# A two-layer hybrid decoder on one core: parameters loaded behind the eighth block of x, the first four blocks singly, and separate accumulators for the last group's row halves

## The chip, the cores and the metric

The kernel runs on one core of a Trainium2 chip. The metric is the device time of one execution in microseconds (us); of several runs the median is given. Engines are called as in the profile: PE (TensorE) with its weight loads PEld, DVE (VectorE), ACT (ScalarE), POOL (GpSimd), and SP, whose queue issues most of the DMAs.

## The reference

Two layers, each of 256 tokens of width 2048, all in float32. A layer is one wide input projection, three mixers on its columns, one output projection, and a LayerNorm of the residual sum:

```
for l in range(DEPTH):                          # DEPTH = 2
    u = x @ w_in[l]                             # 2048 -> 6080 columns
    (cb, cc, ch, cg, cq, ckv, kpe, mg, rcols, rg) = _split(u, IN_SIZES)
    y_conv = _short_conv_branch(cb, cc, ch, cg, conv_w[l])
    y_mla  = _mla_branch(cq, ckv, kpe, mg, ..., cos, sin)
    y_rwkv = _rwkv7_branch(rcols, rg, rwkv_mu[l], ...)
    mix = jnp.concatenate([y_conv, y_mla, y_rwkv], axis=-1)
    x = _layer_norm(DEEPNORM_ALPHA * x + mix @ w_out[l], ln_g[l], ln_b[l])
```

The RWKV branch first mixes each column with the token before it, `xs = cols + (shift(cols) - cols) * mu`, which needs the parameters `mu`.

## The kernel before, in words

Every product is made from two parts of each operand: a rounded "hi" (ACT copies the float32 value to fp32r) and a rest "lo" (DVE subtracts). `split_in` makes the pair; `split_w` does it for a weight block and appends the two instructions to the list `splits`. A product is then hi·hi, hi·lo and lo·hi (`mm3`, lines 341 to 343, or lines 441 and 443 where the hi and lo of x lie side by side and one matmul of 512 columns does two of the three).

The input projection is done in groups of 512 columns (`MAIN`: k, a, r, v, ...). In layer 0 the first group, k, is loaded with x: the 16 blocks of x (128 rows of the transposed x, 256 columns) lie in memory beside the 512 columns of k's weights, so one block of a `first` tile is 128 x 768 values, 384 KB. `STEPS` says which blocks make one load; `load_first` issues the load on SP's queue, and splits the x part, and `split_w` the weight part. In the first group these splits are chained in order on ACT and on DVE (`in_turn`). The `first` tiles lie in pool s8 of nine slots, four of which hold the split x; a tile waits for a free slot. Then come the groups a, r, v and so on, each in two halves: `in_group` takes one accumulator per half, makes 32 pairs of matmuls (L441, L443) into it, and evacuates it with an ACT copy and a DVE add.

Accumulators come from `acc`: pool pp in PSUM, tag "acc", two buffers of two banks each. The group k takes one, the first half of a the other, and the second half of a whichever is released first: k's, when the four `shift_mix` of `rwkv_k` have read it (tile kx, one ACT and one DVE instruction each), or the first half's own, when it is evacuated.

`shift_mix` needs parameters: `pars` (loaded) and `pc` (four DVE instructions made from it in `load_params`, here for both layers). `load_constants` loads `pars`, `cs`, `posi` and `ones` from POOL's queue, behind a one-element POOL copy that reads the last `first` tile, so that they start when that has landed.

The output projection (`out_proj`) has four groups of 512 columns. The last one is done in column halves i = 0 and 1 and row halves h = 0 and 1 (128 tokens each). In layer 0, `po[i][h]` for both h lay in one accumulator tile, one bank each: column half 0 is done for both h and then added to the residual; of column half 1, first h = 0 is multiplied, added (`add`) and its LayerNorm begun (`root`), then h = 1.

A planner writes the order of each engine's instructions (`schedule_with_timeline_sim=True`): it runs a model of time, takes at each point the ready instruction of the highest priority (`high_priority` raises it), and assigns buffers as they come free in that model. `after(a, b)` forces that a stands behind b. Within `tick`, DVE instructions of the mixers are also held behind a weight split further on (`gates`, by the counters `used` and `splits`).

Of the kernel before, what the change touches and what calls it, by code (L numbers as in the profile page):

```python
# [14 lines left out]
ALU = mybir.AluOpType  # L15
# [36 lines left out]
Q_CONV, Q_QG, Q_KVG, Q_MUR, Q_MUWA, Q_MUK, Q_MUV = 0, 12, 16, 18, 22, 23, 27  # L52
Q_W0, Q_A0, Q_KK, Q_KA, Q_RK, Q_GNG, Q_GNB, Q_LNG, Q_LNB = 31, 35, 39, 43, 47, 51, 55, 59, 75
# [58 lines left out]
def hybrid_layers(ctx: ExitStack, tc: tile.TileContext, x, positions, xT, w_in, w_out, w_uq, w_ukv, par, wa_in, gb_in,  # L112
# [13 lines left out]
    gates, splits = {}, []  # L126
# [18 lines left out]
    V, A, G, T = Gated(nc.vector, "V"), Gated(nc.scalar, "A"), nc.gpsimd, nc.tensor  # L145

    def after(inst, earlier):

        tc.add_manual_dep(inst.ins, earlier.ins.name,
                          mybir.DependencyInfo(mybir.DependencyClass.NoSync, mybir.DependencyReason.DATA),  # L150
                          reason="loads no earlier than needed")
# [9 lines left out]
    ones = cp.tile([P, 2 * P], F32R, tag="ones", name="ones")  # L161
# [5 lines left out]
    def load_constants(x):  # L167

        last = G.tensor_copy(pars[0:1, 0, 0:1], x[0:1, 0:1])
        for to, src in ((pars, par), (cs, cst), (posi, positions[0:1, :].to_broadcast([P, S]))):  # L170
            load = nc.gpsimd.dma_start(to, src)
            after(load, last)
            last = load
        o32 = c4("ones32", (P, 2 * P))
        load = nc.gpsimd.dma_start(o32, sums)
        after(load, last)
        V.tensor_copy(ones, o32)
        loaded.append(load)

    def zeros(rows):  # L180

# [2 lines left out]
    params, loaded, mark = [], [], {}  # L184
# [4 lines left out]
    def s4(name, shape=(P, 4, S), dt=F32):  # L189
        return slot("s4", name, shape, N4, dt)  # L190

    def c4(name, shape=(P, 4, S), dt=F32):
        return slot("c4", name, shape, NC4, dt)

    def s8(name, shape=(P, 8, S), dt=F32):
        return slot("s8", name, shape, N8, dt)


    def pair(name):
        return s8(name, (P, 2, 4, S), F32R)  # L200
# [4 lines left out]
    def split_in(hi, lo, src):  # L205
        a = A.copy(hi, src)
        v = V.tensor_tensor(lo, src, hi.bitcast(F32), ALU.subtract)
        if not params:
            in_turn("A", a)
            in_turn("V", v)  # L210
        return a, v
# [1 line left out]
    xres = x  # L213
    xs = [pair(f"x0_{g}") for g in range(4)]

    STEPS = [(0, 1), (1, 1), (2, 2), (4, 2), (6, 2), (8, 2), (10, 2), (12, 2), (14, 2)]

    def load_first(k0, n):

        t = s8(f"first{k0}", (P, n, S + 512))  # L220
        in_turn(1, nc.sync.dma_start(t, xT[:, k0:k0 + n, :]))
        with tc.high_priority():
            to, at = xs[k0 // 4], k0 % 4
            split_in(to[:, 0, at:at + n, :], to[:, 1, at:at + n, :], t[:, :, 0:S])
        if k0 == 14:
            load_constants(t[:, 0, :])
        return t[:, :, S:].rearrange("p k (i c) -> p i k c", i=2)

# [2 lines left out]
    def in_turn(queue, load):  # L231
        if queue in turn:
            after(load, turn[queue])
        turn[queue] = load
# [13 lines left out]
    def load_params(l):  # L248
        pq = pars[:, l, :]
        pc = cp.tile([P, 29], F32, tag=f"pc{l}", name=f"pc{l}")  # L250
        V.tensor_scalar(pc[:, 0:13], pq[:, Q_MUR:Q_MUR + 13], -1.0, 1.0, ALU.mult, ALU.add)
        V.tensor_scalar(pc[:, 13:21], pq[:, Q_W0:Q_W0 + 8], 0.5, None, ALU.mult)
        V.tensor_scalar(pc[:, 21:25], pq[:, Q_KA:Q_KA + 4], 0.5, None, ALU.mult)
        V.tensor_scalar(pc[:, 25:29], pq[:, Q_KA:Q_KA + 4], -0.5, 1.0, ALU.mult, ALU.add)
        col = lambda j: pq[:, j:j + 1] if j < NQ else pc[:, j - NQ:j - NQ + 1]
        return dict(col=col, om=NQ - Q_MUR, hw=NQ + 13, ha=NQ + 17, hk=NQ + 21, ok=NQ + 25)

# [95 lines left out]
    def acc(name):  # L353

        return pp.tile([P, 2, 512], F32, tag="acc", name=name)
# [21 lines left out]
    def wide_steps(l):  # L377
        return [(k, 2) for k in range(0, NKC, 2)] if l else STEPS

# [23 lines left out]
    def weights(name, k0):  # L403
        while len(asked) < LOOK:
            asked.append(load())
        load()
        return ready.pop((name, k0))
# [805 lines left out]
    def ln_rows(l):  # L1213

        t = sm.tile([P, 2, 16], F32, tag="lnp", name=f"lnp{l}", bufs=1)
        load = nc.gpsimd.dma_start(t, gbp[l])
        after(load, loaded[0])
        hi = sm.tile([P, 2, 16], F32R, tag="lnh", name=f"lnh{l}", bufs=1)
        lo = sm.tile([P, 2, 16], F32R, tag="lnl", name=f"lnl{l}", bufs=1)
        V.tensor_copy(hi, t)  # L1220
        V.tensor_tensor(lo, t, hi.bitcast(F32), ALU.subtract)
        rows = dr.tile([5, D], F32R, tag=f"lnr{l}", name=f"lnr{l}")
        for i, src in enumerate((hi[:, 0], lo[:, 0], hi[:, 0], hi[:, 1], lo[:, 1])):
            nc.gpsimd.dma_start(rows[i].rearrange("(p i) -> p i", p=P), src)
        return rows

    def out_proj(l, ms, xres, last, begin, lnr):
# [52 lines left out]
        def part1(at, n):  # L1280
            z = zs[0][:, 1, at:at + n]
            return V.scalar_tensor_tensor(z, z, rstd[:, 1:2], gs[0][:, 1, at:at + n], ALU.mult, ALU.add)
# [59 lines left out]
        for g in range(4):  # L1342
            xr = c4(f"xr{l}_{g}", (P, 2, 512))
            after(nc.scalar.dma_start(xr, xres[0, :, g * 512:(g + 1) * 512].rearrange("(h p) c -> p h c", p=P)), begin)
            zs.append(xr)
            gt = s4(f"gb{l}_{g}", (P, 2, 512))
            after(nc.scalar.dma_start(gt, gb_in[l:l + 1, :, g * 512:(g + 1) * 512].to_broadcast([P, 2, 512])), begin)
            gs.append(gt)
            if g < 3:
                pa = acc(f"po{l}_{g}")  # L1350
                po = [pa[:, h, :] for h in range(2)]
                for k0 in ORDER:
                    ws = [weights(f"wo{l}_{g}", k0 + k) for k in (0, 2)]
                    for h in range(2):
                        part(po, h, 512, ws)
                for h in range(2):
                    add(po[h], g, 0, 512, h, g)
                continue
            po, held = [], {}
            for i in range(2):  # L1360
                pa = acc(f"po{l}_{g}_{i}")
                po.append([pa[:, h, 0:256] for h in range(2)])
                held[i] = []
                for k0 in ORDER:
                    held[i].append(weights(f"wo{l}_3_{i}", k0))
                    if not last and i == 0:
                        for h in range(2):
                            part(po[i], h, 256, held[0][-1:])
                if not last and i == 0:
                    for h in range(2):  # L1370
                        add(po[i][h], g, 0, 256, h, 3)
            cts = []

            def turn_row(h):
                ct, m = row(h)
                cts.append(ct)
                return m

            first_rows = {AT[last][0]: lambda: turn_row(0),
                          AT[last][1]: lambda: [norm(0, g_, cts[0])[0] for g_ in range(4 if last else 1)][-1]}  # L1380
            for h in range(2):
                for i in range(2):
                    if not last and i == 0:
                        continue
                    part(po[i], h, 256, held[i], first_rows if h and i else {})
                    add(po[i][h], g, i * 256, 256, h, 3 + i)
                mark.setdefault(l + 1, []).append(root(h))
            if not last:
                xs += [pair(f"x{l + 1}_{g}") for g in range(1, 4)]
            keep_warm()  # L1390
            if last:
                turn_row(1)
                part1(256, 256)
                nc.scalar.dma_start(rows(0)[:, 1], zs[0][:, 1])
                for g_ in range(1, 4):
                    norm(1, g_, cts[1], ((0, 512),) if g_ < 3 else ((0, 256), (256, 256)))
            else:
                turn(1, 0, ((0, 2),))
                t = turn(0, 0, hold=mark[l + 1][1])
                after(part0(256, 256), mark[l + 1][1])  # L1400
                mark[l + 1][1] = t
                part1(256, 256)
                nc.gpsimd.dma_start(rows(0), zs[0])
                turn(1, 0, ((2, 2),))
                turn_row(1)
                run(rest(cts))
                tick()
# [3 lines left out]
    for l in range(L):  # L1411
        u, t = {}, {}
# [55 lines left out]
```

## Time and profile before

| | |
|---|---|
| median of 3 runs | 908.29 us (908.03 to 909.82) |
| the profiled execution | 909.28 us |
| its span in the trace | 907.5 us |
| PE busy | 893.1 us, 98% of the span |
| DVE, ACT, POOL busy | 687.5, 486.1, 24.6 us |
| TensorE clock granted, mean | 0.994 |

The profiled execution lies 1.78 us above its span, and 0.99 us above the median. "Busy" for PE counts the matmuls whatever their clock; a stage at the half clock is busy twice as long.

### The profile page before, as it was taken

The numbers are of one execution on the slowest core, as the hardware profiler recorded it, in microseconds if no ns is written. First come the engines' busy times: TensorE is split into PE (matmuls) and PEld (weight loads), VectorE is DVE, ScalarE is ACT, GpSimd is POOL, SyncE is SP. The second block draws the span as 40 slices with busy tenths as digits, with TensorE's granted clock in tenths as the row PEclk, the third lists the DMA queues.
The fourth block names the chain that finished last, engine by engine and source line by source line (L and its number), as shares of the span: only waits on it lengthen the run. The fifth ranks groups of instructions, "written<-read, shape, count | busy, mean of one in ns | idle before, by whom it ended". The sixth has DMA issues, their size and how long they took to land.

```text
span 907.5 us, 16003 instructions
## 1 busy us (share of the span) xinstructions
PE 893.1 (98%) x6314; PEld 786.7 (87%) x6314; DVE 687.5 (76%) x1166; ACT 486.1 (54%) x752; POOL 24.6 (3%) x47
## 2 busy tenths in 40 slices
PE   8899999999999999999999999999999999999996
PEld 8788888888889888888898888888888998988896
DVE  7677988986558987476775889799765699875665
ACT  6577546444447666544246874564444575765430
POOL 2120000000000000000020000000000000000000
PEclk9989999999999999999999999999999999999999
DMA  9755674666535654696576456646654456547832
GB/s 373 222 139 161 185 208 130 187 197 177 161 111 165 193 161 118 205 325 204 171 225 194 136 190 191 170 124 204 196 173 141 123 158 209 163 118 239 315 119 93
DMA packets 65100, 164.98 MB, mean 182 GB/s; under 512 B 15286, under 2 KB 23782, under 8 KB 65014
## 3 DMA queue, kind: packets, MB, share of 16 engines
q1 hardware_dynamic: 57264, 150.36, 54.4%
q10 hardware_dynamic: 5072, 9.57, 3.0%
q0 software_dynamic: 2688, 4.03, 1.6%
q8 instruction: 49, 0.80, 0.4%
q14 instruction: 27, 0.22, 0.1%
HBM read 158.61 MB, written 5.32 MB: 181 GB/s over the span
## 4 chain that ended last, share of the span: by engine, by line
PE 95%; DVE 2%; ACT 1%; DMA 1%; issue 0%; DVEq 0%; SPq 0%; ACTq 0%
PE po L341 7%; PE u_mg L441 7%; PE po L343 7%; PE po L342 6%; PE u_a L441 4%; PE u_cc L441 3%; PE u_cg L441 3%; PE u_mg L443 3%; PE u_v L441 3%; PE u_cb L441 3%; PE u_ch L441 3%; PE u_cq L441 3%; PE u_rg L441 3%; PE u_r L441 3%; PE u_rg L443 2%; PE u_cg L443 2%
## 5 line engine op out<-in xcount | busy, mean ns | idle before, releaser
L138 DVE TENSOR_TENSOR lo_wo<-w_wo,hi_wo 128x1024 fp32r<-128x1024 f32 x57 | 69.1, 1222 | 45.0 <-ACT hi_wo L138 44.1
L138 ACT CAST hi_wo<-w_wo 128x1024 fp32r<-128x1024 f32 x57 | 59.3, 1050 | 60.1 <-PE po L343 29.9
L441 PE MATMUL u_mg<-x,hi_mg 128*128 128x512 f32 x256 | 90.0, 396 | 0.0
L443 PE MATMUL u_mg<-x,lo_mg 128*128 128x256 f32 x256 | 71.4, 280 | 0.0
L441 PEld LDWEIGHTS u_mg<-x,hi_mg 128*128 128x128 f32 x256 | 47.9, 188 | 10.8
L441 PE MATMUL u_a<-x,hi_a 128*128 128x512 f32 x128 | 48.1, 415 | 3.1 <-DVE u_a L138 3.1
L443 PEld LDWEIGHTS u_mg<-x,lo_mg 128*128 128x128 f32 x256 | 48.3, 189 | 0.2
L341 PE MATMUL po<-hi_wo,ma 128*128 128x512 f32 (+1 forms) x128 | 46.7, 365 | 0.0
L343 PE MATMUL po<-hi_wo,ma 128*128 128x512 f32 (+1 forms) x128 | 46.5, 363 | 0.0
L342 PE MATMUL po<-lo_wo,ma 128*128 128x512 f32 (+1 forms) x128 | 46.4, 363 | 0.0
L138 ACT CAST hi_mg<-w_mg 128x1024 fp32r<-128x1024 f32 x32 | 33.6, 1049 | 23.8 <-PE u_mg L441 12.5
L441 PE MATMUL u_cc<-x,hi_cc 128*128 128x512 f32 x128 | 46.2, 403 | 0.0
L441 PE MATMUL u_cg<-x,hi_cg 128*128 128x512 f32 x128 | 46.0, 401 | 0.0
L441 PE MATMUL u_cq<-x,hi_cq 128*128 128x512 f32 x128 | 45.4, 395 | 0.0
L441 PE MATMUL u_ch<-x,hi_ch 128*128 128x512 f32 x128 | 45.3, 399 | 0.0
L441 PE MATMUL u_cb<-x,hi_cb 128*128 128x512 f32 x128 | 45.3, 399 | 0.0
L441 PE MATMUL u_v<-x,hi_v 128*128 128x512 f32 x128 | 45.3, 399 | 0.0
L441 PE MATMUL u_rg<-x,hi_rg 128*128 128x512 f32 x128 | 45.3, 394 | 0.0
L441 PE MATMUL u_r<-x,hi_r 128*128 128x512 f32 x128 | 45.1, 394 | 0.0
L138 DVE TENSOR_TENSOR lo_mg<-w_mg,hi_mg 128x1024 fp32r<-128x1024 f32 x32 | 38.8, 1222 | 6.0 <-ACT hi_mg L138 4.4
L343 PE MATMUL u_k<-x,lo_k 128*128 128x256 f32 x128 | 36.9, 288 | 0.8 <-DVE lo_k L138 0.8
L138 DVE TENSOR_TENSOR lo_rg<-w_rg,hi_rg 128x1024 fp32r<-128x1024 f32 x16 | 19.6, 1223 | 23.2 <-ACT hi_rg L138 23.2
(417 smaller groups left out, 2819.5 us busy)
## 6 DMA issues: line engine op xcount, KB each, us to landing
w_wo<-in_w_out_dram SPq DMA_DIRECT2D x64, 512.0 KB, 4.3
w_mg<-in_w_in_dram SPq DMA_DIRECT2D x32, 512.0 KB, 4.0
w_a<-in_w_in_dram SPq DMA_DIRECT2D x16, 512.0 KB, 4.5
w_r<-in_w_in_dram SPq DMA_DIRECT2D x16, 512.0 KB, 3.7
w_v<-in_w_in_dram SPq DMA_DIRECT2D x16, 512.0 KB, 3.7
w_cq<-in_w_in_dram SPq DMA_DIRECT2D x16, 512.0 KB, 3.8
w_cc<-in_w_in_dram SPq DMA_DIRECT2D x16, 512.0 KB, 4.0
w_ch<-in_w_in_dram SPq DMA_DIRECT2D x16, 512.0 KB, 3.7
```

The source lines that it names most:

```text
L138: inst = call(*args, **kwargs)
L341: m = T.matmul(o, lh, rh, start=first, stop=False, skip_group_check=True)
L342: T.matmul(o, lh, rl, start=False, stop=False, skip_group_check=True)
L343: T.matmul(o, ll, rh, start=False, stop=last, skip_group_check=True)
L441: T.matmul(ps[:, b, :].rearrange("p (i t) -> p i t", i=2), hi[:, k, c], x2, start=k0 + k == 0, stop=False, skip_group_check=True)
L443: T.matmul(ps[:, b, 0:S], lo[:, k, c], x2[:, 0, :], start=False, stop=k0 + k == NKC - 1, skip_group_check=True)
```

## The change

`STEPS` loads blocks 2 and 3 singly: ten loads in place of nine. `load_constants` is called with the load of blocks 6 and 7 in place of the last one. The copy that makes `ones` moves from there into `load_params`, where the five DVE instructions are put behind the DVE split of the last of the ten weight blocks; the first instruction on the LayerNorm parameters (`lnh`) is put behind the next split. In layer 0 the last group's column half 1 takes a second accumulator for its row half 1.

```diff
-        V.tensor_copy(ones, o32)
-        loaded.append(load)
+        loaded.extend((load, o32))
...
-    STEPS = [(0, 1), (1, 1), (2, 2), (4, 2), (6, 2), (8, 2), (10, 2), (12, 2), (14, 2)]
+    STEPS = [(0, 1), (1, 1), (2, 1), (3, 1), (4, 2), (6, 2), (8, 2), (10, 2), (12, 2), (14, 2)]
...
-        if k0 == 14:
+        if k0 == 6:
             load_constants(t[:, 0, :])
...
-        V.tensor_scalar(pc[:, 0:13], pq[:, Q_MUR:Q_MUR + 13], -1.0, 1.0, ALU.mult, ALU.add)
-        V.tensor_scalar(pc[:, 13:21], pq[:, Q_W0:Q_W0 + 8], 0.5, None, ALU.mult)
-        V.tensor_scalar(pc[:, 21:25], pq[:, Q_KA:Q_KA + 4], 0.5, None, ALU.mult)
-        V.tensor_scalar(pc[:, 25:29], pq[:, Q_KA:Q_KA + 4], -0.5, 1.0, ALU.mult, ALU.add)
+        vs = [V.tensor_scalar(pc[:, 0:13], pq[:, Q_MUR:Q_MUR + 13], -1.0, 1.0, ALU.mult, ALU.add),
+              V.tensor_scalar(pc[:, 13:21], pq[:, Q_W0:Q_W0 + 8], 0.5, None, ALU.mult),
+              V.tensor_scalar(pc[:, 21:25], pq[:, Q_KA:Q_KA + 4], 0.5, None, ALU.mult),
+              V.tensor_scalar(pc[:, 25:29], pq[:, Q_KA:Q_KA + 4], -0.5, 1.0, ALU.mult, ALU.add)]
+        if l == 0:
+            vs.append(V.tensor_copy(ones, loaded[1]))
+        for v in vs:
+            after(v, splits[len(STEPS) - 1][1])
...
-        V.tensor_copy(hi, t)
+        after(V.tensor_copy(hi, t), splits[len(STEPS)][1])
...
-                po.append([pa[:, h, 0:256] for h in range(2)])
+                pb = pa if last or i == 0 else acc(f"po{l}_{g}_2")
+                po.append([pa[:, 0, 0:256], pb[:, 1, 0:256]])
```

## Rows read from the trace of the kernel before

**Rows 1.** The page, busy time of each engine over the whole span.

```profile
PE 893.1 (98%) x6314; PEld 786.7 (87%) x6314; DVE 687.5 (76%) x1166; ACT 486.1 (54%) x752; POOL 24.6 (3%) x47
```

**Rows 2.** The waits of PE over the whole span: who waited for whom, us in total, times, the longest.

```profile
PE u_a L441 <- DVE u_a L138: 3.1, 1, 3.1
...
PE u_k L343 <- DVE lo_k L138: 0.8, 1, 0.8
...
PE po L341 <- DVE xr L138: 0.5, 1, 0.5
PE pq L341 <- ACT vt L138: 0.5, 2, 0.2
```

**Rows 3.** Stretches at the start of the program: from:to, length, busy us and instructions of each engine, the clock granted to TensorE (1.00 is 2.4 GHz), the busy share of the DMA engines, GB/s.

```profile
10.00:20.00 10.00, 10.00 (x84) 10.00 (x85) 9.63 (x12) 8.36 (x11) 2.38 (x4) 1.00 1.01 414
...
43.00:44.00 1.00, 0.00 (x0) 0.00 (x0) 1.00 (x3) 0.98 (x3) 0.00 (x0) 0.86 0.69 283
44.00:45.00 1.00, 0.51 (x1) 0.50 (x2) 0.97 (x4) 0.99 (x2) 0.00 (x0) 0.50 0.44 74
...
50.00:51.00 1.00, 1.00 (x5) 0.86 (x5) 0.12 (x1) 0.85 (x1) 0.36 (x1) 0.73 1.01 279
```

**Rows 4.** The timeline of the first blocks of x on ACT, DVE and PE (start, duration, engine, line, what; in brackets the idle time before and what ended it). Tile x is the split x, hi_k and lo_k the split weights.

```profile
4.19 0.40 ACT L138 CAST x<-first 128x256 fp32r<-128x256 f32 x1 [2.16 <-DMA first<-in_xT_dram]
4.50 0.61 ACT L138 CAST hi_k<-first 128x512 fp32r<-128x512 f32 x1
5.14 0.69 DVE L138 TENSOR_TENSOR lo_k<-first,hi_k 128x512 fp32r<-128x512 f32 x1
...
7.04 0.62 ACT L138 CAST x<-first 128x512 fp32r<-128x512 f32 x1 [0.97 <-DMA first<-in_xT_dram]
8.65 1.22 DVE L138 TENSOR_TENSOR lo_k<-first,hi_k 128x1024 fp32r<-128x1024 f32 x1 [0.26 <-ACT hi_k L138]
8.89 0.28 PE L342 MATMUL u_k<-x,hi_k 128*128 128x256 f32 x1
9.93 0.39 PE L343 MATMUL u_k<-x,lo_k 128*128 128x256 f32 x1 [0.76 <-DVE lo_k L138]
...
10.53 1.22 DVE L138 TENSOR_TENSOR lo_k<-first,hi_k 128x1024 fp32r<-128x1024 f32 x1
```

**Rows 5.** DMAs: for the `first` loads the least, median and longest time from issue to landing; for the last of the four parameter loads KB and us to landing.

```profile
DMA to landing us min/median/max: 3.4/6.8/9.6
...
ones<-in_sums_dram POOLq DMA_DIRECT2D x1, 128.0 KB, 6.3
```

**Rows 6.** The timeline of POOL: the copy behind which the parameters are issued, and the last of the four issues.

```profile
18.40 0.93 POOL L169 COPY pars<-first 1x1 f32<-1x1 f32 x1 [3.56 <-DMA first<-in_xT_dram]
...
21.43 0.54 POOL L175 DMA_DIRECT2D ones<-in_sums_dram x1
```

**Rows 7.** The timeline of DVE in layer 0, around the first half of group a.

```profile
32.47 0.68 DVE L138 TENSOR_SCALAR pc<-pars 128x13 f32<-128x13 f32 x8
33.05 0.28 DVE L138 CAST ang<-posi 128x256 f32<-128x256 int32 x1
33.93 1.23 DVE L138 TENSOR_TENSOR lo_a<-w_a,hi_a 128x1024 fp32r<-128x1024 f32 x1 [0.59 <-ACT hi_a L138]
...
35.54 0.47 DVE L138 SCALAR_TENSOR_TENSOR kx<-u_k,pars,kx 128x255 f32<-128x255 f32 x1
...
44.35 0.48 DVE L138 SCALAR_TENSOR_TENSOR kx<-u_k,pars,kx 128x255 f32<-128x255 f32 x1
```

**Rows 8.** The same of layer 1.

```profile
483.47 1.22 DVE L138 TENSOR_TENSOR lo_a<-w_a,hi_a 128x1024 fp32r<-128x1024 f32 x1 [1.66 <-ACT hi_a L138]
484.62 0.47 DVE L138 SCALAR_TENSOR_TENSOR kx<-u_k,pars,kx 128x255 f32<-128x255 f32 x1
...
493.10 0.48 DVE L138 SCALAR_TENSOR_TENSOR kx<-u_k,pars,kx 128x255 f32<-128x255 f32 x1
```

**Rows 9.** The timeline of PE: group a in layer 0 (its first matmul behind group k, the last of its first half, the first of its second half, the first of group r), then the same of layer 1 (without the last of the first half).

```profile
30.17 0.28 PE L443 MATMUL u_a<-x,lo_a 128*128 128x256 f32 x1
...
41.13 0.28 PE L443 MATMUL u_a<-x,lo_a 128*128 128x256 f32 x1
44.49 0.79 PE L441 MATMUL u_a<-x,hi_a 128*128 128x512 f32 x1 [3.08 <-DVE u_a L138]
...
59.39 0.39 PE L441 MATMUL u_r<-x,hi_r 128*128 128x512 f32 x1
...
482.31 0.40 PE L441 MATMUL u_a<-x,hi_a 128*128 128x512 f32 x1
...
493.63 0.50 PE L441 MATMUL u_a<-x,hi_a 128*128 128x512 f32 x1
...
505.77 0.39 PE L441 MATMUL u_r<-x,hi_r 128*128 128x512 f32 x1
```

**Rows 10.** The timeline of DVE and PE at the end of layer 0: the residual sums of column half 0 (two) and of column half 1, row half 0, and the last matmul of row half 0 and the first of row half 1.

```profile
437.33 0.74 DVE L138 SCALAR_TENSOR_TENSOR xr<-xr,po 128x256 f32<-128x256 f32 x2
441.82 0.42 DVE L138 SCALAR_TENSOR_TENSOR xr<-xr,po 128x256 f32<-128x256 f32 x1 [2.43 <-PE po L343]
...
441.51 0.28 PE L343 MATMUL po<-wlwo,ma 128*128 128x256 f32 x1
442.30 0.38 PE L341 MATMUL po<-hi_wo,mc 128*128 128x256 f32 x1 [0.51 <-DVE xr L138]
```

## The prediction

> **What bounds the kernel.** I read the busy times first: PE is busy for 98% of the span and no other engine for more than 76% [rows 1]. So a gain must come out of PE's few stops, or out of stretches in which it runs slowly, and where nothing else gives way each such microsecond comes off the end. The waits of PE come next: the longest is 3.1 us in group a of layer 0, and two smaller ones are 0.8 us in the first group, k, and 0.5 us in the output projection of layer 0 [rows 2]. The change has a part for each of the three places. Then the clock by stretches: it is full until PE stops in group a, falls to 0.86 in the microsecond from 43, stands at 0.50 (1.2 GHz) when PE resumes, and returns to full only within the microsecond from 50 [rows 3]. The stop of group a therefore costs about twice what the waits show. Last I read the timelines at the three places, and layer 1, where the parameters have long been loaded, as a model of what layer 0 would look like.
>
> **Part 1: blocks 2 and 3 singly.** PE issues the second matmul of block 2 at 8.89 and should issue the third 0.12 us later (84 matmuls in 10 us [rows 3]); it issues it at 9.93, behind the lo_k of blocks 2 and 3 together, which runs from 8.65 to 9.87 [rows 4]. Lost: 0.92 us. The chain before it: the double load has landed by 7.04, ACT splits x (0.62), then the weights, then DVE. The first block is ready at 4.19 and the double one, two blocks further, at 7.04: three blocks in 2.85 us, 0.95 each, with the DMA engines full [rows 3, 4]. Landing singly, block 2 would be there at about 6.1 and block 3 at 7.05. With the durations of single blocks [rows 4], ACT is through with block 2 at 6.1 + 0.3 + 0.6 = 7.0 (0.3 being the distance at which one cast follows the other) and DVE at 7.1 + 0.7 = 7.8; block 3 follows at 8.0 and 8.75. PE wants block 2 at 8.65 and block 3 twelve matmuls later, at 10.1. Both are ready. Next late are blocks 4 and 5: PE, no longer stopped, needs their first lo_k at 8.65 + 24 x 0.12 + 0.24 = 11.77, and it is ready at 10.53 + 1.22 = 11.75 and a signal later: 0.05 to 0.1 us. Bounds: nothing (the loads don't come sooner) to 0.92; I take 0.85.
>
> A tenth load also shifts the slots: blocks 6 and 7 now wait for the tile of block 0, freed when its lo_k ends at 5.83 [rows 4]. The least time from issue to landing is 3.4 us [rows 5], and for a double load one block more, 4.35 us: 10.2. At the pace of the full stream, four blocks behind 7.04, they land at about 10.8 in any case; so this is hidden, by half a microsecond.
>
> The Trainium skill speaks against this part: its page "DMA: Bandwidth & Descriptors", section "Bandwidth", says to make loads of a MiB and more, since smaller ones get a lower share of the peak. The two 384 KB loads at the head of this trace show no such loss: 0.95 us per block with them, which is the 414 GB/s of the full stream [rows 3]. If the rule held here, blocks 2 and 3 would come later, and this part would give nothing; that is the third rival's price below.
>
> **Part 2: parameters behind the eighth block.** Before, POOL's copy runs when the last x has landed, at 18.40; the last of the four issues behind it is at 21.43, and `ones` lands 6.3 us later, at 27.7 [rows 5, 6]. Now the copy waits for blocks 6 and 7, at about 10.8, 7.6 us earlier: `ones`, the last, would land near 20.1. The five DVE instructions stand behind the tenth lo_k. It ends near 21.2 (the double block that was there at 7.04 was through at 9.87 [rows 4], so 2.8 us behind 18.4); DVE would hardly wait; where it does, what queues behind it are the lo_a splits, which PE first wants when group k ends (30.17 [rows 9], less part 1: 29.3). The parameters (0.68 MB by their shapes, 1.7 us of a full stream at 414 GB/s [rows 3]) now go beside the last blocks of x. PE, after part 1, comes to the last two blocks 24 x 0.12 us before the end of group k, at 26.4. Against the lo_k at 21.2 that is a slack of 5, and 1.7 us more are hidden in it. If that cover were gone, each us would cost one.
>
> What they release: before, the instructions on `pars` run on DVE at 32.47, behind the fourth lo_a, and the four kx follow one for each lo_a from the fifth on, at 35.54 to 44.35 [rows 7]. The second half of group a starts at 44.49, having waited since 41.25 for an accumulator [rows 9]. In layer 1 the first kx stands behind the fourth lo_a, at 484.62, and the last ends at 493.58; the second half starts at 493.63 almost without a stop [rows 8, 9]. One lo_a is 2.8 us: the parameters made layer 0 one step late, and that is the stop. From the first matmul behind group k to the first of group r it is 29.22 us in layer 0 (with one matmul, 0.23 us, done ahead) and 23.46 in layer 1 [rows 9]. So the full price of the stop is 5.99 us: 3.24 of standing still (41.13 + 0.12 to 44.49), and 2.75 of matmuls at the half clock [rows 3].
>
> With parameters in time layer 0 should have layer 1's order. The difference is the rope tables, built only in layer 0, whose DVE instructions (0.28 us for `ang`) [rows 7] fall into the same gaps; one in front of the last kx leaves a stop of 0.3 us or so. PE stood still for 0.76 us before 9.93 [rows 4], and from 10 to 20 the clock was 1.00 [rows 3]; so a small rest stays small. Bounds: nothing (kx still a step late) to 6.0; I take 5.75, near layer 1's row.
>
> The Trainium skill's "TensorE: Matmul & The Clock Gate", section "What's actually happening", says that activity releases a throttle and idleness restores it; the fall from 1.00 to 0.50 during the stop agrees. A sum without it would hold 3.0 us here in place of 5.75.
>
> `lnh`, behind the next split (24 us now), needs a POOL load issued right after `ones`, there by about 20: nothing. The DVE gates keep their distance, as `used` and `splits` both grow by one.
>
> **Part 3: separate accumulators.** The first matmul of row half 1 should start at 441.51 + 0.12 = 441.63; it starts at 442.30, just after the DVE sum over row half 0 (441.82 to 442.24), although that reads the other bank [rows 10]. With a buffer of its own it waits only for the sums of column half 0, over at 438.07 [rows 10]. That is 0.67 us; the row half's LayerNorm chain then moves up with PE. The next layer's group k gets the buffer that row half 0 leaves at 442.24, while row half 1's 48 matmuls are still to come. Bounds: 0 (the wait is of another kind) to 0.67; I take 0.65.
>
> **Sum.** 0.85 + 5.75 + 0.65 = 7.25 us. Against the profiled execution: 909.28 - 7.25 = 902.03; against the median, 0.99 lower, 908.29 - 7.25 = 901.04. Downstream work moves up as a whole: layer 1 runs from group a on with hardly a stop, at the faster start.
>
> **The rivals.**
>
> *One step late still.* The planner's order goes by its own model of time. If that puts the first kx behind the fifth lo_a again (PE now reaches that point 0.85 us sooner), the stop and the half clock stay. Only parts 1 and 3 count: 908.29 - 1.5 = 906.8. For it: layer 0 has the rope work, and layer 1's margin is 0.05 us. Against: in layer 1 the same code has the step right.
>
> *The parameters block DVE: slower.* The five instructions stand at a fixed place; if `ones` lands late, every lo_a waits. PE wants the first lo_a at 29.3, 1.2 us of DVE behind `pc`, so a landing after about 27.8 costs PE 1 us each, and with a stop like group a's the half clock, 2.75 us. The gain of 7.25 is used up by a landing 4.5 us later, 32.3; one at 34.5 gives 910.5. Against: that is 20 us after issue, twice the longest of the x loads, 9.6 [rows 5].
>
> *Single loads are no faster.* Part 1 gives nothing: 901.9.
>
> *The planner writes another order elsewhere.* Accumulators, slots and order after 60 us may change with the model's times. Against: the only other wait of PE listed with these, on vt, is at most 0.2 us long [rows 2]. But one new stop such as group a's costs 6 us: 907; a second one makes it slower, 913.
>
> **Chances and numbers.** My forecast, with all three parts, 0.70: 901.0, between 900.5 (the upper bounds give 908.29 - 0.92 - 6.0 - 0.67 = 900.7, less the 0.26 by which the fastest run lies below the median) and 902.3 (a rest of a microsecond in group a). One step late 0.13, parameters late 0.03, single loads no faster 0.05, another order 0.09 (903 to 913). The range is 900.0 to 906.8: below it leaves half a microsecond for what lies around the span, which differed by more between the runs; above it reaches to the first rival and leaves out its upper half, the late parameters, and half of the other orders. A measurement of this kernel can tell 0.2%, 1.8 us, from no change: below 906.5 is faster. Faster: 0.70 + 0.05 + 0.03 of the first rival + 0.03 of other orders = 0.81; the same: 0.10 + 0.02 = 0.12; slower: 0.07.
>
> **What would show it.** The wait of u_a is gone or under half a microsecond; the clock is 1.00 in every microsecond from 40 to 52; group r starts near 52.6 in place of 59.4; the first kx stands behind the fourth lo_a. No wait of u_k on lo_k above 0.1 us. At the end of layer 0, no gap between the row halves. If group r is earlier but the end isn't, another order has given it back; if the stop in group a is there in full, the first rival holds; if DVE idles in front of `pc`, the second.

## The result and the profile after

| | before | after |
|---|---|---|
| median of the runs | 909.06 us (908.03 to 910.03, 4 runs) | 903.47 us (903.14 to 903.67, 4 runs) |
| ratio, with its 95% interval | | 0.9938 (0.9921 to 0.9956) |
| the profiled execution, time / span | 909.28 / 907.5 | 903.67 / 901.9 |

The changed kernel is faster by 0.6%, 5.6 us. That lies inside the range of the prediction, and 2.5 us above its 901.0; it is outside the narrower 900.5 to 902.3 that the prediction gave for all three parts at work. The kernel before has one run more here, of 910.03, and so its median is 0.8 above the one shown ahead of the prediction.

The places where the time went are found by the first matmul of each part in the two traces (of group a the first one behind group k, as in [rows 9]). All are us from the start of the span; `lw` is the kernel's last matmuls, four in one row, and the time is that row's start.

| | group k, layer 0 | group a | group r | group k, layer 1 | last `lw` |
|---|---|---|---|---|---|
| before | 5.17 | 30.17 | 59.39 | 453.37 | 901.07 |
| after | 5.30 | 30.90 | 54.19 | 447.72 | 895.36 |

So group a became 5.93 shorter (29.22 to 23.29), and the stretch from group r to layer 1 became 0.45 shorter (393.98 to 393.53), but group k became 0.60 longer (25.00 to 25.60). It also began 0.13 later, and what comes after layer 1's start is the same within 0.06. Together: 5.93 + 0.45 - 0.60 - 0.13 + 0.06 = 5.71, the distance between the two `lw`.

The page after, to be read against [rows 1]: PE's work is the same 6314 matmuls, but it is busy for 2.8 us less, since none of group a's runs at the half clock now.

```profile
PE 890.3 (99%) x6314; PEld 784.4 (87%) x6314; DVE 687.7 (76%) x1168; ACT 485.9 (54%) x754; POOL 25.1 (3%) x47
```

The waits of PE over the whole span (total us, times, longest), against [rows 2]: the 3.1 of `u_a` and the 0.5 of `po` are gone. The 0.8 of `u_k` has not gone: two waits for lo_k and one for hi_k stand in its place, 1.5 together.

```profile
PE u_k L346 <- DVE lo_k L138: 1.0, 2, 0.8
...
PE u_k L344 <- ACT hi_k L138: 0.5, 1, 0.5
```

The stretches that [rows 3] show of before: the clock is 1.00 in each, and PE works through where it stood still.

```profile
43.00:44.00 1.00, 1.00 (x8) 0.86 (x7) 1.00 (x3) 0.98 (x3) 1.00 (x2) 1.00 0.81 226
44.00:45.00 1.00, 1.00 (x7) 0.90 (x6) 1.00 (x2) 0.99 (x2) 0.95 (x2) 1.00 1.09 281
50.00:51.00 1.00, 1.00 (x7) 0.86 (x7) 1.00 (x2) 0.99 (x2) 0.00 (x0) 1.00 0.76 307
```

The timeline after, on the engines of [rows 4, 6, 7, 9, 10]:

```profile
6.83 0.41 ACT L138 CAST x<-first 128x256 fp32r<-128x256 f32 x1 [0.65 <-DMA first<-in_xT_dram]
8.54 0.41 ACT L138 CAST x<-first 128x256 fp32r<-128x256 f32 x1 [0.78 <-DMA first<-in_xT_dram]
10.65 0.62 ACT L138 CAST x<-first 128x512 fp32r<-128x512 f32 x1 [1.19 <-DMA first<-in_xT_dram]
...
12.51 1.01 POOL L169 COPY pars<-first 1x1 f32<-1x1 f32 x1 [12.06 <-DMA first<-in_xT_dram]
...
23.00 1.23 DVE L138 TENSOR_TENSOR lo_k<-first,hi_k 128x1024 fp32r<-128x1024 f32 x1 [0.26 <-ACT hi_k L138]
24.14 0.38 DVE L138 TENSOR_SCALAR pc<-pars 128x13 f32<-128x13 f32 x4
...
31.61 0.48 DVE L138 SCALAR_TENSOR_TENSOR kx<-u_k,pars,kx 128x255 f32<-128x255 f32 x1 [1.44 <-ACT kx L138]
...
38.96 0.48 DVE L138 SCALAR_TENSOR_TENSOR kx<-u_k,pars,kx 128x255 f32<-128x255 f32 x1
...
41.98 0.40 PE L444 MATMUL u_a<-x,hi_a 128*128 128x512 f32 x1
...
436.61 0.28 PE L346 MATMUL po<-wlwo,ma 128*128 128x256 f32 x1
436.73 0.28 PE L344 MATMUL po<-hi_wo,mc 128*128 128x256 f32 x1
```

The first three rows are blocks 2 and 3, and then 4 and 5 together. Block 2 is there at 6.83, only 0.21 before the double load of blocks 2 and 3 was [rows 4]; block 3 is there at 8.54, 1.7 us behind it and 1.5 later than before. With the first part of the change, block 3 is late in this execution. The next rows are the second part: `pc` stands at 24.14, right behind the tenth lo_k, with no idle time before it; the last of the four kx starts at 38.96, where it was 44.35; and the second half of group a starts at 41.98 without a stop. The last two rows are the third part: the row halves follow each other in 0.12 us.

### The profile page after: what moved, and what is told of

Its sections match the earlier page's. It is cut to its first block, busy times and chain, and to the rows that moved or that the text cites. A ratio compares the mean times of both kernels' runs of the same rounds, so it can differ in the third digit from the quotient of the medians.

```text
span 901.9 us, 16013 instructions
## 1 busy us (share of the span) xinstructions
PE 890.3 (99%) x6314; PEld 784.4 (87%) x6314; DVE 687.7 (76%) x1168; ACT 485.9 (54%) x754; POOL 25.1 (3%) x47
## 4 chain that ended last, share of the span: by engine, by line
PE 95%; DVE 2%; DMA 1%; ACT 1%; issue 0%; SPq 0%; DVEq 0%; ACTq 0%
PE po L344 7%; PE u_mg L444 7%; PE po L345 7%; PE po L346 7%; PE u_cc L444 3%; PE u_cg L444 3%; PE u_mg L446 3%; PE u_cb L444 3%; PE u_ch L444 3%; PE u_v L444 3%; PE u_a L444 3%; PE u_cq L444 3%; PE u_r L444 3%; PE u_rg L444 3%; PE u_rg L446 2%; PE u_cg L446 2%
## 5 line engine op out<-in xcount | busy, mean ns | idle before, releaser
L444 PEld LDWEIGHTS u_mg<-x,hi_mg 128*128 128x128 f32 x256 | 47.9, 188 | 10.8
L444 PE MATMUL u_a<-x,hi_a 128*128 128x512 f32 x128 | 45.5, 398 | 0.0
```

What stands on the lines that cost most here:

```text
L444: T.matmul(ps[:, b, :].rearrange("p (i t) -> p i t", i=2), hi[:, k, c], x2, start=k0 + k == 0, stop=False, skip_group_check=True)
```

## The experiments

Three theories came out of this. The **first**: the prediction's parts 2 and 3 hold, and part 1 is worth nothing, since single loads come no faster. The **second**: part 1 gives what was forecast, and something else is lost. The **third**, on part 2 alone: the stop costs its 3.1 us everywhere, but the half clock behind it does not follow in every execution, so that the profiled execution of before was a dear one. The runs came in three batches, each on one chip with runs of the kernel before on that chip; comparisons of times stay inside a batch where nothing else is said. The kernel before was at 908.15 in the first (a), 908.07 in the second (b), and 908.63 in the third (c).

### Part 2 undone: the parameters late again

```diff
-        if k0 == 6:
+        if k0 == 14:
             load_constants(t[:, 0, :])
```

> The changed kernel with its parameters loaded behind the last block of x again. Theory: the first kx stands a step later, PE stops 3.1 us in group a and runs at the half clock for some 6 us after it: 5.5 to 6 us above the changed kernel's, 909.2. Rival (order and fixed places brought the gain, not the time of the load): within 1 us of the changed kernel's, 903.5 to 904.5.

Measured: 907.24 median (905.91 to 909.0, 11 runs), ratio 0.9991. Nearly the whole gain is gone, though the time is 2 us below the 909.2 that was expected. The longest wait of PE:

```profile
PE u_a L444 <- DVE u_a L138: 3.1, 1, 3.1
```

The clock by stretches:

```profile
43.00:44.00 1.00, 0.00 (x0) 0.00 (x0) 1.00 (x3) 0.98 (x2) 0.00 (x0) 1.00 0.53 213
44.00:45.00 1.00, 0.77 (x4) 0.68 (x5) 0.85 (x4) 0.99 (x2) 0.05 (x1) 1.00 0.77 106
```

DVE and PE around group a:

```profile
32.22 0.68 DVE L138 TENSOR_SCALAR pc<-pars 128x13 f32<-128x13 f32 x8
...
35.28 0.48 DVE L138 SCALAR_TENSOR_TENSOR kx<-u_k,pars,kx 128x255 f32<-128x255 f32 x1
...
44.23 0.50 PE L444 MATMUL u_a<-x,hi_a 128*128 128x512 f32 x1 [3.08 <-DVE u_a L138]
```

The stop is back in full, 3.08 us, with `pc` and kx a step later, as in [rows 7, 9]. That the parameters' late landing caused it is thereby shown. But the clock is 1.00 in the microsecond in which [rows 3] had 0.50, although PE stood still for as long. Group a takes 26.60 us here, against 29.22 in the trace of before and 23.29 in that of after. So this one pair of differences separates the two terms of the forecast: 3.3 us for the stop and 2.6 for the half clock, and this execution paid only the first.

How often the second is paid is told by the mean granted clock of the runs. Of the 47 runs of the kernel before in the three batches, 9 have a clock of 0.997 and lie at 906.45 to 906.93; the other 38 have 0.994 to 0.996 and lie at 907.81 to 910.42. Of the 11 runs of this kernel, the three at 0.997 and more took 905.91 to 906.12, the eight at 0.996 and less 907.0 and more. The changed kernel's 9 runs all have 0.997 or 0.998. The mean is a rough sign only, since the clock also falls at the end of each trace: the execution profiled of the kernel with one accumulator (below) has 0.996, with 0.54 in its last 7 us and 1.00 until then. The times bear the division out, with nothing between 906.93 and 907.81; of the kernel before itself no execution without the fall was profiled.

### Keeping PE busy in the stop

To the kernel before, 13 matmuls that nothing uses are added behind the first half of group a, where PE would stand still. Nothing is left out.

```diff
-            ps = acc(f"u_{name}{l}_{i}")
+            ps = fill(m) if (l, name, i) == (0, "a", 1) else None or acc(f"u_{name}{l}_{i}")
...
+    def fill(behind):
+        pz = pm.tile([P, 512], F32, tag="m", name="pfill")
+        for _ in range(13):
+            after(T.matmul(pz, xs[3][:, 0, 0, 0:P], xs[3][:, 0, 0:2, :], start=True, stop=True), behind)
+        return acc("u_a0_1")
```

> The kernel before, with 13 matmuls into an unused accumulator in front of the second half of group a, so that PE works through most of the 3.1 us in which it stood still; they add nothing to the output. The last runs showed the same stop followed by a stretch at the half clock in one execution (907.5 us of span) and by none in another (904.8), and times of kernels with the stop spread over 3 to 4 us. Theory (the spread and a part of the stop's price are the clock's fall, which comes in some executions): the second half starts when it did, the clock stays at 1.00, and all runs lie within 0.7 us, at 906.5 to 907.2. Rival (the spread has another cause): a median near 908.1 and runs spread over 3 us as before.

Measured: 908.28 (907.84 to 910.92, 12 runs), ratio 1.0008 (0.9997 to 1.0019): no gain in the median. PE around the filler:

```profile
41.81 3.12 PE L1415 MATMUL pfill<-x 128*128 128x512 f32 x13
45.06 0.50 PE L441 MATMUL u_a<-x,hi_a 128*128 128x512 f32 x1
...
57.30 0.39 PE L441 MATMUL u_r<-x,hi_r 128*128 128x512 f32 x1
```

The filler did its work: group a takes 26.57 us (30.73 to 57.30), 2.65 less than in the trace of before, with the same first half and the same late second half. Ten of the twelve runs have a clock of 0.997 or 0.998, where 9 of 47 had it without the filler. But the run did not get shorter. In this profile group k took 25.65 in place of 25.00, since blocks 2 and 3 reached ACT at 7.62 and not at 7.04 as in [rows 4]; and from group r to `lw` it took 843.65 in place of 841.68: behind the filler the planner wrote another order. That this order costs the 1.97 is inferred and not shown. The two losses, 0.65 and 1.97, use up the 2.65. So the runs show that work in the stop holds the clock in most executions; as a measurement of the price in the median the experiment failed. Two runs at 0.995 (910.86 and 910.92) lost the clock all the same, and where is open.

### Part 3 undone: one accumulator

```diff
-                pb = pa if last or i == 0 else acc(f"po{l}_{g}_2")
+                pb = pa
```

> The changed kernel with part 3 undone (both row halves in one accumulator again). Theory: the 0.5 us wait of PE between the row halves comes back, its first matmul 0.67 us late, and the time is 0.65 us above the changed kernel's, about 904.1. Rival (the wait is of another kind, or the gain was given back behind it): 903.5. The start of the program is the same as in the changed kernel: if single loads slow the stream, blocks 2, 3 and 4 are again there at about 6.8, 8.5 and 10.6 us; if that was chance in one execution, at about 6.1, 7.05 and 8.9, and group k ends 1.6 us sooner.

Measured: 903.66 (903.6 to 904.07, 5 runs), 0.65 above the kernel of the next experiment on the same chip, which has this part and lacks a part that proves to be worth nothing. PE at the end of layer 0:

```profile
435.73 0.28 PE L346 MATMUL po<-wlwo,ma 128*128 128x256 f32 x1
436.52 0.38 PE L344 MATMUL po<-hi_wo,mc 128*128 128x256 f32 x1 [0.51 <-DVE xr L138]
```

The gap is back: 0.79 between the starts in place of 0.12, so 0.67 us. From group r to layer 1 it takes 394.28, and 393.53 in the changed kernel; the kernel before took 393.98. The wait for the other bank was real, and it costs what it shows.

### Part 1 undone, and done alone

The changed kernel with the double load of blocks 2 and 3 (twice, on two chips), the changed kernel itself beside the second, and the kernel before with the ten loads:

```diff
-    STEPS = [(0, 1), (1, 1), (2, 1), (3, 1), (4, 2), (6, 2), (8, 2), (10, 2), (12, 2), (14, 2)]
+    STEPS = [(0, 1), (1, 1), (2, 2), (4, 2), (6, 2), (8, 2), (10, 2), (12, 2), (14, 2)]
```

> The changed kernel with part 1 undone (blocks 2 and 3 in one load). Theory that single loads slow the stream: blocks 2 and 3 are there at 7.0 and blocks 4 and 5 at 8.9, PE stops once for 0.9 us, group k ends at 30.2 in place of 30.9, and the time is 0.7 us below the changed kernel's, 902.8. Rival (the slow stream was chance and singles gain as predicted): 0.85 us above it, 904.3.

> The changed kernel with blocks 2 and 3 in one load, once more beside it. Theory (part 1 costs in place of gaining): 0.3 to 0.6 us below the changed kernel on this chip. Rival (the difference of 0.5 us between the sessions was that of two chips): the same, or 0.3 to 0.85 us above it.

> The changed kernel once more, beside the next three on one chip. If four single loads lose the stream 0.75 us each time, blocks 4 and 5 come at 9.7 to 10.7 us, later than the 8.9 to 9.1 of double loads, and PE stops before them; 903.1 to 903.7.

> The kernel before with part 1 alone. Theory that single loads slow the stream: 0.7 us above the kernel before, about 909.5, with the stop in group a as before. Rival (singles gain as predicted): 0.85 us below it, 907.9.

Measured: with the double load 903.01 (5 runs) on the first chip; on the third 902.94 (902.71 to 903.5, 5 runs), against 902.98 (902.76 to 903.3, 5 runs) of the changed kernel. The single loads alone: 908.08 (11 runs) against 908.15, ratio 0.9995 (0.9986 to 1.0004). Two pairs, and no difference in either beyond the spread of the runs: part 1 is worth nothing that these medians show.

Why is shown by the loads. Of each kernel one stretch, the microsecond from 5 to 6, is shown (the last two columns are the DMA engines' busy share and GB/s), and behind it, for the pair of the third chip, the split of blocks 4 and 5 on ACT. First the stretch in the kernel before, whose blocks 4 and 5 come at 8.93:

```profile
5.00:6.00 1.00, 1.00 (x4) 0.61 (x3) 0.91 (x3) 0.96 (x3) 0.00 (x0) 1.00 1.06 442
```

Then the changed kernel with the double load, on the third chip:

```profile
5.00:6.00 1.00, 1.00 (x4) 0.61 (x3) 0.91 (x3) 0.96 (x3) 0.00 (x0) 1.00 1.04 436
```

```profile
8.94 0.62 ACT L138 CAST x<-first 128x512 fp32r<-128x512 f32 x1 [0.32 <-DMA first<-in_xT_dram]
```

And the changed kernel beside it:

```profile
5.00:6.00 1.00, 1.00 (x4) 0.59 (x3) 0.91 (x3) 0.99 (x3) 0.00 (x0) 1.00 1.00 292
```

```profile
9.77 0.62 ACT L138 CAST x<-first 128x512 fp32r<-128x512 f32 x1 [0.92 <-DMA first<-in_xT_dram]
```

With the third and fourth block loaded singly the DMA engines are just as busy and move a third less in this stretch. It isn't that all packets are slower: in the trace's records of the packets, 83 of the 95 packets of 3 KB that begin in this stretch take 0.12 us, as in the microsecond before, and the other twelve take 0.17 to 0.93. The missing 144 KB are 0.33 us at 436 GB/s; the stretches up to 9 are slower too (409, 390 and 387 against 424, 418 and 436), and blocks 4 and 5 come 0.83 later. From there on both streams keep their pace of 1.87 for two blocks. So the single loads give PE block 2 sooner (6.09 here) and everything from block 3 on later. The stretch has 286 to 304 GB/s in all five traces of kernels with the four single loads in this layout, and 406 to 442 in all five with two; the slow packets in it are 9 to 14 in the former and none or one in the latter. One trace with two single loads, that of the filler, has a late block as well (7.62, above) without this fall in the rate: one packet of it, begun at 4.57, took 0.91 us in place of 0.23. So the doubles are not safe in every execution.

How much this costs differs between executions. Group k takes 25.60 in the first profile of the changed kernel, and 24.71 to 24.92 in the other four traces with these loads; with the double load split whole it takes 25.00 and 25.01 (25.65 with the filler). So the first profile shows the dearest of five executions, and the others a gain of 0.1 to 0.3 there, not the 0.85.

A second thing hid in these traces. In the execution profiled on the third chip, the changed kernel has no wait of `u_k` at all. PE at the start:

```profile
6.29 0.41 PE L344 MATMUL u_k<-x,hi_k 128*128 128x256 f32 x1
6.51 0.41 PE L345 MATMUL u_k<-x,hi_k 128*128 128x256 f32 x1
...
7.93 0.28 PE L346 MATMUL u_k<-x,lo_k 128*128 128x256 f32 x1
```

Its matmuls are 0.21 apart until about 7.7, where the plain pace is 0.12 (the trace's first record of the clock is at 7.8), and so it comes to the late blocks later and finds them ready. Its group k takes 24.83, that of the first profile, which was at full pace by then and stood still for 1.5 us, 25.60. Whether PE crawls or waits, the blocks set the pace there.

### More singles, and a split block by block

Eight single loads and a double load split block by block came next, in the second batch. The eight were expected to make things worse, and did not. From the two the theory was drawn that the six single loads of the third batch tested: what PE waits for is the first double load behind the singles, because a double load is split as a whole and is only of use when its 1.22 us of lo_k are over. Then six or eight single loads remove the wait despite the slower stream, and so does the double load, if its split is cut in two.

```diff
-    STEPS = [(0, 1), (1, 1), (2, 1), (3, 1), (4, 2), (6, 2), (8, 2), (10, 2), (12, 2), (14, 2)]
+    STEPS = [(k, 1) for k in range(8)] + [(8, 2), (10, 2), (12, 2), (14, 2)]
...
-        if k0 == 6:
+        if k0 == 7:
```

> The changed kernel with all of the first eight blocks loaded singly. Theory (each single load behind the second costs the stream 0.2 us): blocks 4 to 7 come at 1.15 us each in place of 0.93, the eighth lands about 1.6 us later than with two singles, and PE stops more often; group k ends 0.5 to 1 us later than with four singles, 904 to 904.5. Rival (the loss of 0.7 us comes once, where the stream passes from single to double loads): the loss moves behind the eighth block, PE has a lead by then, and the time is 902.5 to 903.

Measured: 901.89 (901.83 to 901.92, 4 runs), ratio 0.9932 (0.9917 to 0.9946), below both expectations. PE has no wait of `u_k`.

```diff
-    STEPS = [(0, 1), (1, 1), (2, 1), (3, 1), (4, 2), (6, 2), (8, 2), (10, 2), (12, 2), (14, 2)]
+    STEPS = [(k, 1) for k in range(6)] + [(6, 2), (8, 2), (10, 2), (12, 2), (14, 2)]
```

> The changed kernel with blocks 4 and 5 loaded singly too. With eight single loads the stream lost as much as with four, and PE didn't stop. Theory (what PE waits for is the first double load behind the singles, which is there only as a whole): PE has no stop in group k, 1.2 to 1.6 us below the changed kernel, 901.9. Rival (the lead came from blocks 6 and 7 too): PE stops before blocks 6 and 7 and the time is 902.5 to 903.

Measured: 902.28 (901.82 to 902.84, 5 runs), 0.7 below the changed kernel on that chip, where 1.2 to 1.6 was expected. PE has no wait of `u_k` here either.

```diff
-    STEPS = [(0, 1), (1, 1), (2, 1), (3, 1), (4, 2), (6, 2), (8, 2), (10, 2), (12, 2), (14, 2)]
+    STEPS = [(0, 1), (1, 1), (2, 2), (4, 2), (6, 2), (8, 2), (10, 2), (12, 2), (14, 2)]
...
+        if k0 == 2:
+            return split_singly(t, raw, to, at)
...
+    def split_singly(t, raw, to, at):
+        hi, lo = [wh.tile(list(raw.shape), F32R, tag=g, name=f"{g}_k0_2") for g in ("hi", "lo")]
+        for j in range(2):
+            with tc.high_priority():
+                split_in(to[:, 0, at + j, :], to[:, 1, at + j, :], t[:, j, 0:S])
+            with tc.high_priority(AHEAD):
+                ops = split_in(hi[:, :, j, :], lo[:, :, j, :], raw[:, :, j, :])
+        splits.append(ops)
+        return hi, lo
```

> The changed kernel with blocks 2 and 3 in one load again, but split on ACT and DVE block by block (four casts and four subtractions in place of two and two). Theory (single loads slow the stream by some 0.7 us, single splits are what PE's stop needed): the double load is there at 7.0 to 7.2, the lo_k of block 2 is ready at about 8.9 and of block 3 at about 9.9, PE's stop of 0.6 to 0.9 us is gone, and the time is 0.6 us below that of the double load split at once (903.0): 902.4. Rival (the double load, not its split, is what was late): 903.0.

Measured: 902.24 (901.7 to 903.32, 6 runs), with the double load of the kernel before. The split of blocks 2 and 3 on DVE there:

```profile
7.91 0.69 DVE L138 TENSOR_TENSOR lo_k<-first,hi_k 128x512 fp32r<-128x512 f32 x1
8.86 0.69 DVE L138 TENSOR_TENSOR lo_k<-first,hi_k 128x512 fp32r<-128x512 f32 x1
```

The lo_k of block 2 is ready at 8.60 and that of block 3 at 9.55, where both were ready at 9.87 [rows 4], and PE wants that of block 2 at 9.01 (8.89 + 0.12) by the prediction's reading. Group k takes 23.85, 23.84 and 23.98 with eight singles, six singles and the fine split, against 25.01 with the double load split whole: 1.0 to 1.2 us, a little more than the 0.92 that the prediction gave part 1 at the most. All three have medians below both kernels, 902.28 against 902.98 in the pair on one chip. The eight singles and the fine split have only the kernel before (908.07) beside them on their chip; the changed kernel's other medians are 902.98 and 903.47.

The rate of the loads in the eight singles, and then its blocks 2 to 4 on ACT:

```profile
5.00:6.00 1.00, 0.98 (x3) 0.50 (x2) 0.91 (x3) 0.98 (x3) 0.00 (x0) 1.00 1.03 252
```

```profile
6.20 0.41 ACT L138 CAST x<-first 128x256 fp32r<-128x256 f32 x1
8.34 0.41 ACT L138 CAST x<-first 128x256 fp32r<-128x256 f32 x1 [1.22 <-DMA first<-in_xT_dram]
9.29 0.41 ACT L138 CAST x<-first 128x256 fp32r<-128x256 f32 x1
```

The loss is there too: block 3 comes at 8.34, more than two microseconds behind block 2, and then the blocks come 0.95 apart again. So it is a loss of one place, not of each single load, nor of the passage from single to double loads.

### Another layout of x

One candidate was the order of the rows in memory. Here `xT` lies block by block, so that a single load reads one closed piece.

```diff
-        in_turn(1, nc.sync.dma_start(t, xT[:, k0:k0 + n, :]))
+        in_turn(1, nc.sync.dma_start(t, xT[k0:k0 + n].rearrange("k p c -> p k c")))
```

> The changed kernel with the array of x and the first weights laid out block by block, so that a load of one block reads 384 KB in one piece, in place of 128 rows of 3 KB that lie 48 KB apart; a double load then has two rows of 3 KB per partition. All else, and the order of the instructions, is as in the changed kernel. Theory (the singles' loss comes of how their rows lie in memory): 3 KB packets stay at 0.12 us, blocks 2, 3 and 4 with 5 come at 6.1, 7.0 and 8.9 to 9.1, and the time is 0.7 to 1.3 us below the changed kernel. Rival (it comes of how the loads are issued and queued): the packets of the fourth us are slow again, at 0.15 us or more, and the time is the same.

Measured: 903.36 (902.14 to 903.44, 5 runs), with the same order of instructions as the changed kernel. The same stretch:

```profile
5.00:6.00 1.00, 1.00 (x5) 0.89 (x5) 0.81 (x2) 0.80 (x2) 0.00 (x0) 1.00 0.99 295
```

295 GB/s: the fall in the rate is there, so the layout of the rows is not its cause. The blocks behind it come otherwise, though. The first is there at 3.80, 0.3 to 0.5 sooner than in the other traces, blocks 2 and 3 at 6.14 and 7.14, where the prediction had them, and blocks 4 and 5 at 9.16 in place of 9.77. Group k takes 24.32 in this profile, which is the fastest of the five runs; the median is no better than the changed kernel's. The cause of the slow packets stays open.

## Why the prediction was right or wrong

**Which stop bounds the kernel, and that it would go: right.** The parameters' landing made group a one step late; putting it back (the first experiment) brings back the stop of 3.08 us and nearly all of the time. What PE waited for, in the end, was the other one of the two accumulators. DVE's sum that evacuates the first half of group a, in the trace of before and then in that of after:

```profile
43.75 0.68 DVE L138 TENSOR_TENSOR u_a<-u_a,u_a 128x512 f32<-128x512 f32 x1
```

```profile
44.74 0.68 DVE L138 TENSOR_TENSOR u_a<-u_a,u_a 128x512 f32<-128x512 f32 x1
```

Before, it ended at 44.43 and the second half began at 44.49, while the last kx ran until 44.83 [rows 7, 9]: with kx a step late the second half got the accumulator of the first. After, the second half begins at 41.98, before that sum, so it has that of group k, whose last kx is over at 39.44.

The steps in between held except for their hours: POOL's copy ran at 12.51, not 10.8, since the blocks came later; DVE met `pc` behind the tenth lo_k without a wait, at 24.14 and not 21.2. The first kx stands behind the third lo_a, one earlier than in layer 1 and in the prediction's list of signs. Group a takes 23.29, and layer 1's 23.46 was the model. Group r began at 54.19 and not at 52.6, and the whole of that difference is group k: 30.90 where 29.3 was forecast.

**The size of part 2: wrong for the median, right for the profile.** The 3.24 for standing still and the 2.75 for the half clock, 5.99 in all, are both in the traces (group a became 5.93 shorter). But the sum took "2.75 of matmuls at the half clock" from one execution and set it against the median. The same stop leaves the clock at 1.00 in the traces of two kernels (the one with late parameters and the one with single loads alone), and 9 of 47 runs of the kernel before have the mean clock and the time of an execution without the fall. In the medians of the first chip part 2 is worth 4.3 to 4.4: 908.15 - 903.01 is parts 2 and 3, 5.14, of which 908.08 - 907.24 = 0.84 is part 3; and 908.15 - 903.66 = 4.49 is parts 1 and 2, of which 0.07 is part 1. So the term was 1.4 too large. The Trainium skill's "TensorE: Matmul & The Clock Gate", section "What's actually happening", says of the warming up that its length differs between runs, because the chip's look at activity is not tied to the kernel's instructions. This case's traces agree: the first record of the clock is at 5.2 and at 7.8 in two executions of the changed kernel; and the fall behind a stop differs between runs of one program too. The prediction read the half of that section that says that idleness throttles, and the trace that agreed with it.

**Part 1: wrong.** The step that failed is "Landing singly, block 2 would be there at about 6.1 and block 3 at 7.05": it carried the 0.95 us per block of the first two loads on to two more. They came at 6.83 and 8.54 in the first profile, at 6.09 and 7.92 in the one of the third chip. With that, "Next late are blocks 4 and 5 ... 0.05 to 0.1 us" failed: in the first profile they came at 10.65 in place of 8.93, and PE waited 1.2 us for them (the other 0.2 of its waits was for block 0). Value 0 by the medians in place of 0.85. The rival "Single loads are no faster" had this outcome; it had too small a chance. (The first matmul of block 2 in the trace of before is at 8.74, not at the 8.65 of the working; nothing hangs on it.) The rule of the Trainium skill that the prediction weighed there ("DMA: Bandwidth & Descriptors", section "Bandwidth": larger loads get more of the peak) pointed the right way. As it stands it doesn't describe the loss, though: two single loads cost nothing in [rows 3, 4], four cost 0.7 to 0.9 us once (1.7 in the first profile), and twice as many don't cost twice that (the first double load behind eight comes at 14.03, against 13.51 with four and 12.70 with two).

**The slots: wrong, and harmless.** The prediction had blocks 6 and 7 wait for the tile of block 0, as if four of the nine slots were taken by the split x from the start. In the trace of after SP issues seven loads in one go, at the start:

```profile
0.75 3.38 SPq L220 DMA_DIRECT2D first<-in_xT_dram  x7
```

The seventh is the load of blocks 8 and 9; only those behind it wait. In the trace of before it was six loads, up to the same blocks. Nothing came of it in either case.

**Part 3: right.** 0.65 forecast, 0.67 in the gap of the trace, 0.65 and 0.84 in the two differences of medians (the second between kernels whose runs spread over 3 us). The stretch from group r to layer 1 became 0.45 shorter against the kernel before and 0.75 against the kernel with one accumulator.

**The sum.** Too much by 0.85 (part 1) and by 1.4 (part 2's clock term at the median): 2.25 of the 2.5 us by which 901.0 was missed. The rest is less than the medians of one kernel differ by from chip to chip.

## What to carry to other kernels

A stop of the engine that bounds the kernel is priced from the trace for the time that it stands still. What the clock costs behind it is a matter of the execution: before it is set against a median, look at the mean clock of several runs, and take the share of them in which it fell.

Cutting a load finer helps only if what lies behind it is cut as finely and the stream keeps its rate. Here it was the split, done for two blocks as a whole, that made PE wait, and cutting the split alone gave the gain that loading these two blocks singly did not.

Where a consumer late in the program waits on a chain that begins with a load, walk the chain back to what the load itself is queued behind: here it was a copy on POOL that waited for the last x.

## What the runs showed of the hardware

The clock after the same stop of PE, of 3.08 us: down to 0.50 and back only some seven microseconds later in one execution (the kernel before), 1.00 throughout in two others (late parameters; single loads alone); group a takes 29.22 with the fall, 26.60 and 26.47 without it. The runs of one program have both outcomes by their mean clock and time, and no run here shows what decides it.

With four, six or eight single loads of 384 KB at the head of the stream, the microsecond from 5 to 6 has 252 to 335 GB/s at a busy share of 0.93 to 1.05, where with two it has 406 to 442. A few packets of it, 9 to 19, take 0.16 to 1.46 us in place of 0.12. Blocks 4 and 5 come at 9.67 to 10.65 with four, and at 8.84 to 9.49 with two; then the stream has its full pace again. The fall is there with the rows block by block too. Its cause was not found.

The column of the granted clock reads 1.00 from the first microseconds on, but that is for want of a record. The traces' first record of the clock is at 5.2 in the first profile of the changed kernel, at 6.2 in that of the kernel before, and at 7.8 in the one of the third chip, and from there on the distance between matmuls of 256 columns is 0.12, but behind a wait. Ahead of 7.8 it is 0.21 in the last of these, about what it is where the column reads 0.50 (0.22, from 45.08 to 45.30 in the trace of before). So at the very start PE's pace has to be read from the distance between matmuls, and the mean clock doesn't count that stretch.
